# Gate and up projections of the feed-forward sublayers: pairs of inner tiles from seven products of halves, with weight sums formed by ScalarE and an adding DMA

## The chip, the cores and the metric

The kernel runs on one core of a Trainium2 chip. The metric is the time of one execution on the device in microseconds (us). Engines have these names in the profile: PE (TensorE, matmuls), PEld (TensorE's weight loads), DVE (VectorE), ACT (ScalarE), POOL (GpSimd) and SP (SyncE, which issues nearly all DMAs here).

## The reference, cut to what matters

Two layers work on 512 tokens with a model width of 1024. Each layer is a SwiGLU feed-forward sublayer, a token mixer (two kinds of attention and a convolution), and a second SwiGLU sublayer. All is in 32-bit floats.

```python
def swiglu(h, w_up, w_down):
    gate, up = jnp.split(h @ w_up, 2, axis=-1)
    return (jax.nn.silu(gate) * up) @ w_down
...
for l in range(DEPTH):                                   # 2
    mod = (einsum('bd,de->be', silu(c), w_ada[l]) + b_ada[l]).reshape(b, 9, d)
    h = modulate(rmsnorm(x, norm_g[l, 0]), mod[:, 0], mod[:, 1])
    x = x + 0.5 * mod[:, 2][:, None] * swiglu(h, w_ffn_in[l, 0], w_ffn_out[l, 0])
    ...                                                  # token mixer
    h = modulate(rmsnorm(x, norm_g[l, 2]), mod[:, 6], mod[:, 7])
    x = x + 0.5 * mod[:, 8][:, None] * swiglu(h, w_ffn_in[l, 1], w_ffn_out[l, 1])
```

The width inside a feed-forward sublayer is 2816: 22 inner tiles m of 128 channels, each with a gate and an up half. `c` is constant, so `mod` is 72 vectors of 128 channels a layer.

## The kernel before

**Stages.** The program runs the sublayers one after the other. They are called here FFN 1 (with the setup, to about 402 us), mixer 1 (to 994), FFN 2 (to 1370), FFN 3 (to 1745), mixer 2 (to 2331) and FFN 4 (to the end). FFN 2 and FFN 3 follow each other, the last of layer 0 and the first of layer 1.

**A product.** Every operand is kept as two parts, hi and lo, in the format fp32r, and every product is three matmuls into one PSUM bank: hi by hi (L196), weight lo by activation hi (L198), weight hi by activation lo (L200). A feed-forward "unit" is one half (gate or up) of one inner tile m: eight slices k of the width, so 24 matmuls of 512 columns (the tokens), with a 128x1024 block of weights.

**The weights' pipeline.** `plan` yields the keys of the weight blocks in the order of use. `load` lets SP issue the block's DMA into `wr` (512 KB; tag wraw, 3 buffers), makes hi `wh` on ScalarE (L171) and lo `wl` on VectorE (L175), 3 buffers each. `weight` keeps two blocks ahead of the one in use. All of it stands in the program's order: an engine takes its instructions in that order, and a scheduler doesn't move them.

**A feed-forward sublayer.** `norm_h` makes `hh`/`hl` (hi and lo of the normalized input, eight tiles each) at the end of the sublayer before. `head` runs the first three units by halves of the tokens (256 columns). `finish` applies silu on ScalarE (L465), multiplies on VectorE (L466) and splits the product (L190, L191) for the down projection. The inner tiles are taken in three groups (`GROUPS`: 8, 7, 7); after the first tile of the next group the group's down projection runs, eight blocks d, each added to x by `residual` (L420). `tail` does the last group; its last two tiles d run by token halves, so that the next norm lies beside them.

**Other work beside it.** `ada` (L353) makes one vector of `mod` from a 512 KB block: a DMA on SP and one VectorE instruction. 56 of these jobs of layer 0 run in FFN 1, and the 72 of layer 1 belong to FFN 2 (`ada1`), where up to four stand behind each inner tile; in the trace they lie earlier, at about 800 to 990 us in mixer 1, since engines that have nothing else to do there reach them.

Of the kernel before, what the change touches and what calls it, by code (L numbers as in the profile page):

```python
# [13 lines left out]
F32 = mybir.dt.float32  # L14
# [6 lines left out]
P = 128  # L21
T = 512
D = 1024
KD = 8
L = 2
FT = 22
GROUPS = ((0, 8), (8, 15), (15, 22))
# [45 lines left out]
class Trunk:  # L73
    def __init__(self, tc, ctx, io, stop):
# [33 lines left out]
    def plan(self, stop):  # L108
        """Keys of the weight units in the order of their use."""
        n = 0  # L110
        for l in range(L):
            for s in range(3):
# [12 lines left out]
                else:  # L125
                    f = s // 2
                    pend = None
                    if n == 1:
                        yield from (("first", k) for k in range(KD))
                    for m in range(3 if n == 1 else 0, FT):  # L130
                        yield ("in", l, f, m, 0)
                        yield ("in", l, f, m, 1)
                        if pend is not None:
                            yield from (("down", l, f, pend, d) for d in range(KD))
                        pend = {GROUPS[0][1]: 0, GROUPS[1][1]: 1}.get(m + 1)
                    yield from (("down", l, f, 2, d) for d in range(KD))
# [20 lines left out]
    def load(self):  # L157
        key = next(self.keys, None)
        if key is None:
            return  # L160
        nc = self.nc
        src, n = self.source(key)
        kind = key[0]
        raw = self.wp.tile([P, 1024], F32, tag="wraw", name=self.name("wr"), bufs=3)
        hi = self.wp.tile([P, 1024], F32R, tag="whi", name=self.name("wh"), bufs=3)
        lo = self.wp.tile([P, 1024], F32R, tag="wlo", name=self.name("wl"), bufs=3)
        r = raw[:, :n]
        if len(src.shape) == 3:
# [7 lines left out]
        self.loaded.append((key, hi, lo))  # L176
# [222 lines left out]

    def norm_h(self, l, s, k, pb, rng, between=None):  # L400
# [56 lines left out]
    def ffn(self, l, f, ada, cb, stats, nxt, first=None):  # L457
# [3 lines left out]
        start = 0  # L461
# [20 lines left out]
        pend = None  # L482
        early = []
        for m in range(start, FT):
            if m == 0:
                early = self.head(lambda j: self.weight("in", l, f, j // 2, j % 2))
            ps = []
            for j in range(2):
                if early:
                    ps.append(early.pop(0))  # L490
                    continue
                w = self.weight("in", l, f, m, j)
                ps.append(self.bank("mm"))
                self.mmk(ps[j], w, self.h, range(KD), 0, KD - 1)
# [531 lines left out]
```

## Time and profile before

| what | value |
|---|---|
| time of the runs | 2712.62 us median of 3 (2711.9 to 2713.2) |
| span of the profiled execution | 2710.6 us |
| PE busy | 2598.4 us (96%) |
| PEld busy | 2123.6 us (78%) |
| DVE busy | 1612.7 us (59%) |
| ACT busy | 903.2 us (33%) |
| POOL busy | 352.4 us (13%) |
| data moved | 311.27 MB, 115 GB/s on average |

The span runs from the profiled execution's first instruction to its last and is the only time that the profile has of that execution; it is 2.0 us below the median of the runs. Busy shares are averages over stages that differ: the feed-forward sublayers are almost all matmuls, the mixers mix matmuls with much VectorE and GpSimd work. Row groups further down give the stages apart.

### The profile page before, as it was taken

How to read it: one execution, taken by the hardware profiler on the slowest of the kernel's cores; microseconds unless marked ns; L12 is line 12 of the kernel's file. 1: busy time of each engine (PE TensorE's matmuls, PEld its weight loads, DVE VectorE, ACT ScalarE, POOL GpSimd, SP SyncE). 2: the span in 40 equal slices, each digit the busy share in tenths (PEclk: the TensorE clock that was granted, in tenths of full speed). 3: DMA queues.
4: the chain of work that ended last, by engine and by line, in shares of the span. 5: the costliest groups of instructions: out<-in, count | busy, mean ns of one | idle time of the engine just before them, and what ended most of it. 6: DMA issues, size and time to landing. Idle time of an engine off the chain costs nothing.

```text
span 2710.6 us, 31579 instructions
## 1 busy us (share of the span) xinstructions
PE 2598.4 (96%) x12288; PEld 2123.6 (78%) x12288; DVE 1612.7 (59%) x3000; ACT 903.2 (33%) x1490; POOL 352.4 (13%) x289
## 2 busy tenths in 40 slices
PE   7999998689999999999999999977999999999999
PEld 5888887568877788888888888866787778888887
DVE  8883349987868983333353333599878634633333
ACT  3222232245562333222232222322456423422221
POOL 3000004990000000000000000069700000000000
PEclk9999999899999999999999999987999999999999
DMA  7872224222238843223322223221221223222222
GB/s 282 303 286 93 95 92 118 62 62 62 71 101 317 315 166 109 93 90 97 94 86 95 96 90 97 82 70 55 63 67 66 78 93 98 90 93 93 92 95 86
DMA packets 97576, 311.27 MB, mean 115 GB/s; under 512 B 10330, under 2 KB 17242, under 8 KB 97427
## 3 DMA queue, kind: packets, MB, share of 16 engines
q1 hardware_dynamic: 97280, 309.13, 34.3%
q8 instruction: 96, 1.57, 0.2%
q14 instruction: 54, 0.43, 0.1%
q10 hardware_dynamic: 146, 0.14, 0.0%
HBM read 307.09 MB, written 6.06 MB: 116 GB/s over the span
## 4 chain that ended last, share of the span: by engine, by line
PE 83%; DVE 13%; DMA 2%; issue 1%; ACT 1%; SPq 0%; ACTq 0%; DVEq 0%
PE mm L200 24%; PE mm L196 24%; PE mm L198 24%; DVE ca L564 3%; PE mm L634 2%; PE mm L630 2%; PE mm L632 2%; PE s L693 2%; DVE wl L175 2%; DMA ada<-in_w_ada 1%; PE o L762 1%; PE s L735 1%; DVE ada L353 1%; DVE hx L406 1%; DVE rs L235 1%
## 5 line engine op out<-in xcount | busy, mean ns | idle before, releaser
L175 DVE TENSOR_TENSOR wl<-wr,wh 128x1024 fp32r<-128x1024 f32 (+2 forms) x429 | 514.9, 1201 | 475.3 <-ACT wh L171 473.1
L198 PE MATMUL mm<-hh,wl 128*128 128x512 f32 (+1 forms) x2024 | 774.5, 383 | 1.9 <-DVE wl L175 1.8
L196 PE MATMUL mm<-hh,wh 128*128 128x512 f32 (+1 forms) x2024 | 773.2, 383 | 2.4 <-ACT hh L408 2.1
L200 PE MATMUL mm<-hl,wh 128*128 128x512 f32 (+1 forms) x2024 | 767.9, 383 | 6.5 <-DVE hl L411 6.2
L171 ACT ACTIVATE wh<-wr 128x1024 fp32r<-128x1024 f32 (+2 forms) x442 | 444.6, 1006 | 907.6 <-issue 407.2
L200 PEld LDWEIGHTS mm<-hl,wh 128*128 128x128 f32 x2024 | 377.9, 188 | 91.0 <-DVE hl L411 9.7
L198 PEld LDWEIGHTS mm<-hh,wl 128*128 128x128 f32 x2024 | 380.2, 188 | 87.1 <-DVE wl L175 5.4
L196 PEld LDWEIGHTS mm<-hh,wh 128*128 128x128 f32 x2024 | 379.7, 188 | 85.9 <-ACT hh L408 3.5
L196 PE MATMUL mm<-ah,wh 128*128 128x512 f32 (+1 forms) x760 | 288.8, 380 | 0.0
L198 PE MATMUL mm<-ah,wl 128*128 128x512 f32 (+1 forms) x760 | 288.7, 380 | 0.0
L200 PE MATMUL mm<-al,wh 128*128 128x512 f32 (+1 forms) x760 | 288.2, 379 | 0.0
L420 DVE SCALAR_TENSOR_TENSOR x<-mm,res,x 128x512 f32<-128x512 f32 (+1 forms) x124 | 86.2, 698 | 255.3 <-PE mm L200 255.2
L630 PE MATMUL mm<-wh,hh 128*128 128x384 f32 x512 | 188.8, 369 | 39.4 <-DVE v L640 22.2
L175 POOL TENSOR_TENSOR wl<-wr,wh 128x768 fp32r<-128x768 f32 (+1 forms) x13 | 30.5, 2347 | 1456.7 <-ACT wh L171 1456.7
L632 PE MATMUL mm<-wl,hh 128*128 128x384 f32 x512 | 188.1, 367 | 0.0
L634 PE MATMUL mm<-wh,hl 128*128 128x384 f32 x512 | 186.0, 364 | 0.0
L466 DVE TENSOR_TENSOR sil<-sil,mm 128x512 f32<-128x512 f32 x87 | 59.7, 687 | 212.0 <-PE mm L200 210.6
L353 DVE SCALAR_TENSOR_TENSOR ada<-ada,cb 128x1024 f32<-128x1024 f32 x144 | 174.7, 1231 | 17.0 <-DMA ada<-in_w_ada 16.2
L567 POOL TENSOR_TENSOR ca<-ca,prod 128x512 f32<-128x512 f32 x120 | 174.9, 1457 | 9.8
L196 PEld LDWEIGHTS mm<-ah,wh 128*128 128x128 f32 x760 | 143.1, 188 | 30.0
L198 PEld LDWEIGHTS mm<-ah,wl 128*128 128x128 f32 x760 | 143.1, 188 | 29.9
L200 PEld LDWEIGHTS mm<-al,wh 128*128 128x128 f32 x760 | 143.1, 188 | 29.8
(172 smaller groups left out, 2961.6 us busy)
## 6 DMA issues: line engine op xcount, KB each, us to landing
wr<-in_w_ffn_in SPq DMA_DIRECT2D x170, 512.0 KB, 3.3
ada<-in_w_ada SPq DMA_DIRECT2D x144, 512.0 KB, 6.6
wr<-in_w_down SPq DMA_DIRECT2D x64, 448.0 KB, 3.3
wr<-in_w_qkv SPq DMA_DIRECT2D x64, 384.0 KB, 3.2
wr<-in_w_gate SPq DMA_DIRECT2D x48, 512.0 KB, 3.3
wr<-in_w_down SPq DMA_DIRECT2D x32, 512.0 KB, 3.3
wr<-in_w_branch SPq DMA_DIRECT2D x24, 512.0 KB, 3.6
wr<-in_w_u SPq DMA_DIRECT2D x16, 512.0 KB, 3.4
```

Of the source, the lines that this page charges most:

```text
L171: nc.scalar.activation(hi[:, :n], raw[:, :n], AF.Copy)
L175: eng.tensor_tensor(lo[:, :n], raw[:, :n], hi[:, :n].bitcast(F32), op=ALU.subtract)
L196: nc.tensor.matmul(ps[:, rng], w[0][:, wcol], ah[:, rng], start=start, stop=False)
L198: nc.tensor.matmul(ps[:, rng], w[1][:, wcol], ah[:, rng], start=False, stop=False)
L200: nc.tensor.matmul(ps[:, rng], w[0][:, wcol], al[:, rng], start=False, stop=stop)
L353: nc.vector.scalar_tensor_tensor(w, w, 1.0, cb, op0=ALU.mult, op1=ALU.mult, accum_out=self.mod[l][:, e:e + 1])
L420: self.nc.vector.scalar_tensor_tensor(self.x[d][:, rng], ps[:, rng], self.res[l][:, 8 * s + d:8 * s + d + 1], self.x[d][:, rng], op0=ALU.m ...
L564: eng.scalar_tensor_tensor(ca[j], u, w, ca[j], op0=ALU.mult, op1=ALU.add)
L567: eng.tensor_tensor(ca[j], ca[j], prod, op=ALU.add)
L630: nc.tensor.matmul(o, hi[:, hs], w[0][:, ws], start=k == 0, stop=False)
L632: nc.tensor.matmul(o, hi[:, hs], w[1][:, ws], start=False, stop=False)
L634: nc.tensor.matmul(o, lo[:, hs], w[0][:, ws], start=False, stop=k == KD - 1)
```

## The change

The matrix product of two inner tiles (a "pair" j, tiles 2j and 2j+1) is taken as a 2x2 product of blocks: tokens in two halves, the width in two halves of four slices k, and gate against up. It is then formed from seven products of half size and sums (the Winograd form of Strassen's scheme) instead of eight:

- Each product is 2 tiles x 4 slices x 3 parts = 24 matmuls of 256 columns (`product`). A pair had 96 matmuls of 512 columns and has 168 of 256.
- The weight blocks 11, 21, 12, 22 (gate and up, each with the lower and upper half of the width, for both tiles) have 128x1024 elements. Products 1, 2, 3 use blocks 11, 21, 22 as loaded by SP. Products 5, 7, 6, 4 use t1 = 12 - 11, t3 = 12 - 22, t2 = 22 - t1, t4 = 21 - t2. For each of these four `less` writes the negated first operand with ScalarE (L251), and a DMA issued by POOL adds the other block from memory onto it (L252).
- The activations' sums S1 to S4 are made once a sublayer (`sums`, VectorE L555 to L561, splits L267 and L268) from unsplit copies `hq` of the normalized input, which `norm_h` now writes as well (a ScalarE instruction of 256 columns for each tile and half).
- In `pair`, three intermediate values are copied out of PSUM on ScalarE (L599) and three sums are taken on VectorE; then silu (L626, L629), products and splits for both tiles together.
- The products run in the order 1, 2, 6, 7, 5, the next pair's 1, 3, 4. The next pair's blocks are therefore loaded, negated and added during products 7 to 4 of the pair before, or, at a group's end, during the down projection.
- FFN 1 keeps its tiles 0 to 3 as they were and has 9 pairs; FFNs 2 to 4 keep tiles 0 and 1 and have 10 pairs each: 39 pairs in all. The groups are 8, 8 and 6 tiles.
- Space: wraw has 5 buffers instead of 3; t1, t2, `hq` and the `ada` blocks share 4 double buffers with the convolution's tiles. Of the 72 jobs of `ada1`, 40 stay in FFN 2 (up to two after each pair, plain tile or down tile) and 32 move to FFN 3. The split of the convolution's output moves to the end of the mixer.

```diff
-GROUPS = ((0, 8), (8, 15), (15, 22))
+GROUPS = ((0, 8), (8, 16), (16, 22))
+ORDER = (1, 2, 6, 7, 5, 3, 4)
...
+    def block(self, l, f, j, p):
+        if p == 1:
+            self.pairs[j] = b = {}
+            src = {q: self.io["w_up"][l, f, j, i] for i, q in enumerate((11, 21, 12, 22))}
+            for q in (11, 21, 22):
+                b[q] = self.raw()
+                self.nc.sync.dma_start(b[q], src[q])
+            self.less(b, "t1", self.z4k("t"), b[11], src[12])
+            self.less(b, "t3", self.raw(), b[22], src[12])
+            self.less(b, "t2", self.z4k("t"), b["t1"], src[22])
+            self.less(b, "t4", self.raw(), b["t2"], src[21])
+        return self.pairs[j][{1: 11, 2: 21, 6: "t2", 7: "t3", 5: "t1", 3: 22, 4: "t4"}[p]]
+
+    def less(self, b, name, out, a, src):
+        self.nc.scalar.activation(out, a, AF.Copy, scale=-1.0)
+        self.nc.gpsimd.dma_start(out, src, accum_op=ALU.add)
+        b[name] = out
...
+        if s != 1:
+            for half in range(2):
+                if rng in (FULL, HALF[half]):
+                    nc.scalar.activation(self.quarter(k, half), hx[:, HALF[half]], AF.Identity, bias=b)
...
+    def sums(self):
+        tt = self.nc.vector.tensor_tensor
+        a11, a12, a21, a22 = (self.quarters[q] for q in (11, 12, 21, 22))
+        self.S = {}
+        def keep(n, t):
+            self.S[n] = (self.t4k([P, D], F32R, "sh"), self.t4k([P, D], F32R, "sl"))
+            self.split(self.S[n], t)
+        tt(a22, a21, a22, op=ALU.add)
+        tt(a21, a21, a11, op=ALU.subtract)
+        tt(a11, a22, a11, op=ALU.subtract)
+        keep(2, a11)
+        keep(3, a21)
+        keep(1, a22)
+        tt(a12, a12, a11, op=ALU.subtract)
+        keep(4, a12)
...
+    def product(self, l, f, j, p, bank, first):
+        nc = self.nc
+        w = self.weight("up", l, f, j, p)
+        acts = self.operand(p)
+        for mi in range(2):
+            o = bank[:, mi * 256:mi * 256 + 256]
+            for k in range(4):
+                c = slice((mi * 4 + k) * P, (mi * 4 + k + 1) * P)
+                for x, (a, b) in enumerate(((0, 0), (1, 0), (0, 1))):
+                    nc.tensor.matmul(o, w[a][:, c], acts[k][b], start=first and (mi, k, x) == (0, 0, 0),
+                                     stop=(k, x) == (3, 2), skip_group_check=True)
+
+    def pair(self, l, f, j, st, nxt, acts):
...
+        if 1 not in st:
+            run(st, j, 1, "mm")
+        snap("c11")
+        run(st, j, 2, "s")
+        tt(st["c11"], st["c11"], st[2], op=ALU.add)
+        more(6)
+        snap("u2")
+        run(st, j, 7, "s")
+        more(5)
+        snap("c22")
+        tt(st["c22"], st["c22"], st[7], op=ALU.add)
+        later = {}
+        if nxt is not None:
+            run(later, nxt, 1, "mm")
+        more(3)
+        self.product(l, f, j, 4, st[7], False)
...
```

Where the instructions now stand, at two places. First ScalarE's queue in FFN 4. Before, in the steady part, a tile m has two weight splits, one silu and one split of the result:

```order
L465 ACTIVATE sil_3475_20228<-mm_3470_20172 128x512
L171 ACTIVATE wh_3479_20236<-wr_3478_20235 128x1024
L171 ACTIVATE wh_3483_20267<-wr_3482_20266 128x1024
L190 ACTIVATE ah_3476_20231<-sil_3475_20228 128x512
L465 ACTIVATE sil_3486_20297<-mm_3481_20241 128x512
```

Of the change, the stretch from pair 2 to pair 3. Here `wr_3515` is pair 3's block 11, `t_3518` and `t_3520` are its t1 and t2, and `wh_3507`, `wh_3509`, `wh_3513` are the hi parts for pair 2's products 6, 7 and 5:

```order
L599 ACTIVATE c11_3505_21886<-mm_3495_21791 128x512
L224 ACTIVATE wh_3507_21889<-t_3490_21754 128x1024
L251 ACTIVATE t_3518_21983<-wr_3515_21977 128x1024
L224 ACTIVATE wh_3509_21918<-wr_3489_21751 128x1024
L629 ACTIVATE u2_3481_21711<-u2_3481_21711 128x512
L251 ACTIVATE t_3520_21989<-t_3518_21983 128x1024
L267 ACTIVATE ah_3503_21882<-act_3502_21876 128x1024
L224 ACTIVATE wh_3513_21949<-t_3488_21748 128x1024
```

What moved: between the weight splits of one pair there now stand two negations of the next, and the second (`t_3520<-t_3518`) reads what the DMA has added onto the first; the split for product 5 is queued behind it.

Second, the start of FFN 4. On ScalarE, behind the head, `sh` are hi parts of the sums, `wr_3461` is pair 1's block 11, `t_3464`, `t_3466`, `wr_3467` its t1, t2 and t4, and the last row is the hi part for product 6:

```order
L267 ACTIVATE sh_3454_21554<-hq_3434_21360 128x1024
L251 ACTIVATE t_3464_21576<-wr_3461_21570 128x1024
L267 ACTIVATE sh_3456_21559<-hq_3417_21236 128x1024
L599 ACTIVATE c11_3475_21651<-mm_3472_21622 128x512
L267 ACTIVATE ah_3459_21566<-sil_3471_21617 128x512
L251 ACTIVATE t_3466_21582<-t_3464_21576 128x1024
L251 ACTIVATE wr_3467_21585<-t_3466_21582 128x1024
L224 ACTIVATE wh_3477_21654<-t_3466_21582 128x1024
```

On VectorE at the same place, from the last `hl` of the norm on, with the sums on the `hq` tiles and their lo parts `sl`:

```order
L499 SCALAR_TENSOR_TENSOR hl7_97<-hx_3437_21373,shift1_110,hh7_96 128x256
L555 TENSOR_TENSOR hq_3434_21360<-hq_3429_21339,hq_3434_21360 128x1024
L556 TENSOR_TENSOR hq_3429_21339<-hq_3429_21339,hq_3412_21215 128x1024
L228 TENSOR_TENSOR wl_3446_21393<-wr_3444_21390,wh_3445_21392 128x1024
L557 TENSOR_TENSOR hq_3412_21215<-hq_3434_21360,hq_3412_21215 128x1024
L645 TENSOR_TENSOR sil_3458_21563<-sil_3458_21563,mm_3448_21397 128x512
L561 TENSOR_TENSOR hq_3417_21236<-hq_3417_21236,hq_3412_21215 128x1024
L228 TENSOR_TENSOR wl_3469_21589<-wr_3461_21570,wh_3468_21588 128x1024
L268 TENSOR_TENSOR sl_3451_21547<-hq_3412_21215,sh_3450_21546 128x1024
L268 TENSOR_TENSOR sl_3453_21551<-hq_3429_21339,sh_3452_21550 128x1024
```

What moved: t1 takes over the memory of a tile `hq`, so its negation waits until VectorE has read that tile for the last time (the first `sl`), and t2's negation waits for t1's DMA. Before the change VectorE had nothing there between `hl7` and the split of a weight.

## Rows read from the trace of the kernel before

**Rows 1.** The page's first part: span, and busy time of the engines.

```profile
span 2710.6 us, 31579 instructions
PE 2598.4 (96%) x12288; PEld 2123.6 (78%) x12288; DVE 1612.7 (59%) x3000; ACT 903.2 (33%) x1490; POOL 352.4 (13%) x289
```

**Rows 2.** Busy by stretch: us, PE, PEld, DVE, ACT, POOL, clock, DMA share, GB/s.

```profile
994.00:1370.00 376.00, 375.48 (x1736) 307.02 (x1735) 148.32 (x210) 105.33 (x140) 3.16 (x2) 1.00 0.29 93
...
2331.00:2710.60 379.60, 375.22 (x1733) 306.75 (x1731) 142.10 (x186) 99.33 (x130) 2.40 (x1) 1.00 0.28 92
```

**Rows 3.** Waits of PE in FFN 4 (2331 to 2711).

```profile
PE mm L200 <- DVE hl L411: 0.3, 1, 0.3
```

**Rows 4.** Timeline of DVE in FFN 3, down projection.

```profile
1481.23 0.75 DVE L420 SCALAR_TENSOR_TENSOR x<-mm,res,x 128x512 f32<-128x512 f32 x1 [2.64 <-PE mm L200]
...
1486.85 0.75 DVE L420 SCALAR_TENSOR_TENSOR x<-mm,res,x 128x512 f32<-128x512 f32 x1 [3.26 <-PE mm L200]
```

**Rows 5.** Timeline of DVE at the end of FFN 4, by token halves.

```profile
2699.41 0.48 DVE L420 SCALAR_TENSOR_TENSOR x<-mm,res,x 128x256 f32<-128x256 f32 x1 [1.72 <-PE mm L200]
2701.88 0.48 DVE L420 SCALAR_TENSOR_TENSOR x<-mm,res,x 128x256 f32<-128x256 f32 x1 [1.98 <-PE mm L200]
```

**Rows 6.** Timeline of ACT behind the head of FFN 3.

```profile
1387.08 0.92 ACT L408 ACTIVATE hh<-hx,shift 128x256 fp32r<-128x256 f32 x2 [1.05 <-DVE hx L406]
1389.17 1.06 ACT L171 ACTIVATE wh<-wr 128x1024 fp32r<-128x1024 f32 x1 [1.18 <-PE mm L200]
1390.13 0.58 ACT L465 ACTIVATE sil<-mm 128x512 f32<-128x512 f32 x1
1390.61 1.05 ACT L171 ACTIVATE wh<-wr 128x1024 fp32r<-128x1024 f32 x1
```

**Rows 7.** Timeline of DVE behind the head of FFN 3.

```profile
1387.62 0.89 DVE L411 SCALAR_TENSOR_TENSOR hl<-hx,shift,hh 128x256 fp32r<-128x256 f32 x2 [0.19 <-ACT hh L408]
...
1392.00 1.22 DVE L175 TENSOR_TENSOR wl<-wr,wh 128x1024 fp32r<-128x1024 f32 x1
1393.14 0.69 DVE L191 TENSOR_TENSOR al<-sil,ah 128x512 fp32r<-128x512 f32 x1
1393.78 1.23 DVE L175 TENSOR_TENSOR wl<-wr,wh 128x1024 fp32r<-128x1024 f32 x1
```

**Rows 8.** Busy time in a stretch of mixer 1 with many ada loads.

```profile
900.00:950.00 50.00, 50.00 (x215) 40.04 (x214) 46.39 (x74) 15.92 (x21) 0.37 (x3) 1.00 0.89 322
```

**Rows 9.** DMA issues: count, KB each, median us from issue to landing.

```profile
wr<-in_w_ffn_in SPq DMA_DIRECT2D x170, 512.0 KB, 3.3
ada<-in_w_ada SPq DMA_DIRECT2D x144, 512.0 KB, 6.6
...
wr<-in_w_ffn_in SPq DMA_DIRECT2D x8, 384.0 KB, 9.2
```

**Rows 10.** Timeline of PE where the head of FFN 3 ends.

```profile
1391.31 0.28 PE L200 MATMUL mm<-hl,wh 128*128 128x256 f32 x1
1391.42 0.39 PE L196 MATMUL mm<-hh,wh 128*128 128x512 f32 x1
```

**Rows 11.** Timeline of PE in mixer 1, the first matmuls after an idle time.

```profile
492.65 0.66 PE L630 MATMUL mm<-wh,hh 128*128 128x384 f32 x1 [11.42 <-DVE v L640]
493.10 0.53 PE L632 MATMUL mm<-wl,hh 128*128 128x384 f32 x1
...
496.30 0.47 PE L634 MATMUL mm<-wh,hl 128*128 128x384 f32 x1
...
496.78 0.34 PE L632 MATMUL mm<-wl,hh 128*128 128x384 f32 x1
496.96 0.34 PE L634 MATMUL mm<-wh,hl 128*128 128x384 f32 x1
```

**Rows 12.** Busy time in the stretch of these matmuls, columns as in rows 2.

```profile
492.00:496.00 4.00, 3.35 (x11) 3.38 (x12) 4.00 (x14) 0.00 (x0) 3.73 (x4) 0.50 0.35 98
```

**Rows 13.** Weight loads of TensorE, grouped by line and shape.

```profile
L198 PEld LDWEIGHTS mm<-hh,wl 128*128 128x128 f32 x2024 | 380.2, 188 | 87.1 <-DVE wl L175 5.4 <-issue 0.4
```

More of the change, by code (lines that the diff above doesn't have):

```diff
@@ L83, in __init__ @@
         self.uid = 0
+        self.spare = None
+        self.ready = False
+        self.zspare = None
+        self.pairs = {}
         self.keys = self.plan(stop)
+        self.quarters = {}
         self.loaded = deque()
@@ L125, in plan, with ffn_blocks, ffn_plan @@
                 else:
[L126 to L136, printed above, removed]
+                    yield from self.ffn_plan(n, l, s // 2)
                 if n == stop:
                     return
+    def ffn_blocks(self, n):
+        plain = 4 if n == 1 else 2
+        out = [("plain", m) for m in range(3 if n == 1 else 0, plain)]
+        pend = None
+        for j in range(plain // 2, FT // 2):
+            out.append(("pair", j))
+            if pend is not None:
+                out.append(("down", pend))
+            pend = {GROUPS[0][1]: 0, GROUPS[1][1]: 1}.get(2 * j + 2)
+        return out
+    def ffn_plan(self, n, l, f):
+        if n == 1:
+            yield from (("first", k) for k in range(KD))
+        blocks = self.ffn_blocks(n)
+        early = False
+        for (kind, i), nxt in zip(blocks, blocks[1:] + [("end", 0)]):
+            if kind == "plain":
+                yield ("in", l, f, i, 0)
+                yield ("in", l, f, i, 1)
+            elif kind == "down":
+                yield from (("down", l, f, i, d) for d in range(KD))
+            else:
+                for p in ORDER:
+                    if p == 1 and early:
+                        continue
+                    if p == 3 and nxt[0] == "pair":
+                        yield ("up", l, f, nxt[1], 1)
+                    yield ("up", l, f, i, p)
+                early = nxt[0] == "pair"
+        yield from (("down", l, f, 2, d) for d in range(KD))
     def source(self, key):
@@ new lines, in pair, with run, snap, more @@
+    def pair(self, l, f, j, st, nxt, acts):
+        nc = self.nc
+        tt = nc.vector.tensor_tensor
+        def run(st, j, p, tag, first=True):
+            if first:
+                st[p] = self.bank(tag)
+            self.product(l, f, j, p, st[p], first)
+        def snap(name):
+            st[name] = self.t2k(name)
+            nc.scalar.activation(st[name], st[1], AF.Copy)
+        def more(p):
+            self.product(l, f, j, p, st[1], False)
+        if 1 not in st:
[14 more added lines that the diff above has]
+        self.product(l, f, j, 4, st[7], False)
+        act = self.t4k([P, 2, T], F32, "act")
+        halves = [act[:, :, h] for h in HALF]
+        def two(t):
+            return t.rearrange("p (a b) -> p a b", a=2)
+        nc.scalar.activation(st["c11"], st["c11"], AF.Silu)
+        tt(halves[0], two(st["c11"]), two(st[1]), op=ALU.mult)
+        tt(st["u2"], st["u2"], st[7], op=ALU.add)
+        nc.scalar.activation(st["u2"], st["u2"], AF.Silu)
+        tt(halves[1], two(st["u2"]), two(st["c22"]), op=ALU.mult)
+        hi, lo = self.act_tiles("a")
+        self.split((hi, lo), act)
+        for i in range(2):
+            acts[2 * j + i] = (hi[:, i, :], lo[:, i, :])
+        return later
@@ L471, in unit, with more @@
             return lambda d: self.weight("down", l, f, g, d)
+        def more(k):
+            for _ in range(k):
+                if ada:
+                    ada.popleft()(cb)
         if first:
-            start = 3
             banks = [self.bank(t) for t in ("mm", "mm", "mm", "mm", "s", "s")]
```

155 lines of the change are left out of this document (100 added, 55 removed).

## The prediction

> **What bounds the kernel now.** The first view is the page's busy time: PE is busy 2598.4 of 2710.6 us and the other engines far less [rows 1]. Such a share is an average, so the second view is the busy time by sublayer: in FFN 2 PE works 375.48 of 376.00 us, in FFN 4 375.22 of 379.60, at the full clock, while ACT works about 100 us, DVE 142 to 148 and the DMA engines 0.28 of the time [rows 2]. The third is the list of PE's waits: 0.3 us in FFN 4 [rows 3]. The feed-forward sublayers are a gapless stream of matmuls. Each us of PE taken out is gained, as long as nothing else becomes late; each us by which a weight or a sum comes late is lost in full, since nothing covers it.
>
> The profiled execution has no time of its own beside its span, 2710.6; the median of the runs, 2712.6, lies 2.0 above. I work out differences from the trace and take them from the median.
>
> **What is removed.** One `residual` of the down projection follows the next after 1486.85 - 1481.23 = 5.62 us [rows 4], the time of 24 matmuls of 512 columns. In the tail's token halves the step is 2701.88 - 2699.41 = 2.47 us for 7 x 3 = 21 matmuls of 256 columns [rows 5]: 0.1174 us each against 0.2341, just half. A product of 24 costs 24 x 0.1174 = 2.82 us. A pair took 4 x 5.62 = 22.48 and will take 7 x 2.82 = 19.72: 2.76 us less, and for 39 pairs **107.6 us** less. Both counts come from shapes that the trace has; this term is firm.
>
> **What is added, in steady pairs.** By busy time nothing overflows: for each pair ACT does 12 instructions of 128x1024 (seven hi parts, four negations, one split) at 1.0 us and five of 512 columns at 0.5 [rows 6], 14.6 us; DVE eight at 1.15 and five at 0.6 [rows 7], 12.2 us; both under 19.72. DMA: 900:950 moves 322 GB/s at a share of 0.89 [rows 8], so 512 KB occupy all engines for 1.45 us; three plain loads and four adding ones, each counted twice since the target is read too, make 11 x 1.45 = 16.0 of 19.72.
>
> But the order of ACT's queue forms a loop. The second negation of the next pair (t2) needs what the DMA put into t1, and the hi part for product 5 stands behind it. Around the loop: hi part for product 6 (1.0), negate t1 (1.05), DMA (D), negate t2 (1.05), split of the result (1.0), hi part for product 5 (1.0), its lo part (1.15), products 5, 1, 3 (8.45) until the buffer for the next hi part 6 is free: **14.7 + D**. Against 19.72 PE waits once D exceeds 5.0. The loop runs at 15 transitions between pairs (1 to 2, 2 to 3, 3 to 4, 7 to 8 in FFNs 2 to 4; three of FFN 1); at the others one of a group's eight down tiles (5.62 us each) lies between the negations. Loss: 15 x (D - 5.0), not below 0.
>
> **D, the unknown price.** The trace has no adding DMA and none issued by POOL. From below, a plain load of 512 KB: 3.3 us from issue to landing; from above, the slowest load, 9.2 [rows 9]. I start at 3.3, add 1.45 for reading the target and 0.7 for half of another load on the same engines: **D = 5.4**, between the rows 3.3 and 6.6 (the `ada` loads, several in flight), the two nearest.
>
> *A page on this.* The Trainium skill, "Collectives: The Full Stack", section on the bandwidth ceiling (fold count), says that an add in the DMA path costs no computing time, but a second source read (measured ratio 62.28 to 32.35). No run here shows it. By it alone D would be about 3.3 + 1.45 = 4.75, an estimate, and the sum below 2658; I keep the 0.7 of sharing.
>
> **What is added, at the four starts.** Here nothing has run ahead, and the chain is serial. FFN 4, counted from the end of the last `hl` (1388.51 for FFN 3 [rows 7]): DVE does L555 and L556 (2.3), a weight's lo part (3.45), L557 (4.6), a silu product (5.2), L561 (6.35), the lo part of product 1 (7.5), the first lo of a sum (8.65). Then `hq` is free and ACT negates t1 (9.7); it lands at 9.7 + D; t2 negated 10.75 + D, landed 10.75 + 2D; t4 negated, hi and lo part of product 6: **14.0 + 2D**. PE ends the head 1391.42 - 1388.51 = 2.9 us after the last `hl` [rows 7, 10], then runs the fourth unit (5.62) and products 1 and 2 (5.64): ready for product 6 at 14.2. Loss 2D - 0.2. By the same count in the other queues: FFN 2, where t1 waits for the third lo part (2.3 later), 2D + 2.1; FFN 3, with an `ada` instruction between, 2D + 2.6; FFN 1, where tile 3's two units stand between, 2D - 1.6. Sum **8D + 2.9** = 46.1.
>
> Two smaller terms belong to these starts. The extra `hq` instruction on ACT (0.46, as each of the two `hh` [rows 6]) makes ACT's 0.92 a tile as long as DVE's own; its last copies delay the final `hl` by between 0 and eight times 0.46; I take 1.2 for three norms, **3.6**. And PE will stand still for about 10 us: after an idle time of 11.42 [rows 11] the trace shows a granted clock of 0.50 [rows 12], the 1.2 GHz level, with matmuls of 384 columns 0.32 apart, where later ones are 0.18 apart [rows 11]. Some 3.85 us at half speed lose 1.9; four times, **7.6**; nothing if the idle times stay too short for it.
>
> **What is moved.** `ada` blocks now take turns with t1 and t2 for four buffers. While down tiles run, a DMA or negation may wait for a VectorE instruction of `ada`: 0 to 5 us in all, I take **3**. In mixer 1 fewer `ada` jobs compete (900:950 has PE full as it is [rows 8]), but the convolution's late split is added at a place that DVE reaches with work to spare: taken as 0, bounds 2 gained, 4 lost. Five raw buffers and SP's queue cost nothing: loads take 3.3 us [rows 9] against products of 2.82 with two blocks ahead, and only three of seven blocks come through SP.
>
> **Sum.** 107.6 - 46.1 - 3.6 - 7.6 - 15 x 0.4 (6.0) - 3 = 41.3 gained: 2712.6 - 41.3 = **2671**. In general the gain is 107.6 - 17.1 - 8D - 15 x (D - 5.0), the last where D is over 5. D = 3.3 gives 64.1 (2648; 2641 with the clock kept), D = 6.6 gives 13.7 (2699), and nothing is left at D = 7.2.
>
> **Rivals.**
>
> *The adding DMA is cheap* (D up to 4.5, the steady loop never waits): 2636 to 2655. For it: the plain load's 3.3; against it: twice the traffic, and two to three other loads under way at a start.
>
> *The adding DMA is dear, and the change loses.* From D = 7.2 on, the loop and the starts eat up the saved matmuls. At 9.2 the loss is 8 x 9.2 + 17.1 + 15 x 4.2 - 107.6 = 46: 2759. The same comes if its transfers use engines for longer than two plain ones: four times three reads' worth would make (3 + 12) x 1.45 = 21.8 us a pair, over 19.72, 39 x 2.1 = 82 us more. For it: 9.2 and 6.6 in this trace, where loads queue [rows 9]; against it: FFNs use 0.28 of the DMA engines [rows 2], so that there is room.
>
> *The halved matmuls don't halve.* Were the spacing bound by the weight load, 188 ns each [rows 13], a pair would take 168 x 0.188 = 31.6 us, 9.1 more than now: 2712.6 + 39 x 9.1 = 3068. Against it stand 21 such matmuls in 2.47 us, 0.117 apart with a load each [rows 5]. The Trainium skill, "TensorE: Matmul & The Clock Gate", section "Back-to-back issue gap", says that load and matmul together set the spacing, about 81 ns at 128 columns and 131 at 512; by that line (98 at 256, an estimate) half the columns cost 0.75 of the time, and a pair 29.3 us. The trace disagrees: 0.50.
>
> *No change* (within 0.2%, 5.4 us, which is what a measurement of this kernel can tell): D from 7.0 to 7.4, or a smaller D with the mixers a little worse.
>
> **How the numbers follow.** D between 4.5 and 6.1, with the bounds of the small terms: 0.43, time 2655 to 2690, likeliest 2671. Cheap adds (2636 to 2655): 0.18. D near 6.6 (2690 to 2707): 0.13. No change (2707 to 2718): 0.07. Slower: 0.19, of which 0.17 for the dear DMA (a third of it below 2725) and 0.02 for the spacing. The range 2640 to 2730 leaves out about 0.04 below and 0.14 above. The forecast's own range is 2655 to 2690. Faster 0.74, same 0.07, slower 0.19.
>
> **What would show it.** In the profile after: 256-column matmuls about 0.117 apart; PE busy lower by about 108 us; in each sublayer one idle time of some 10 us ahead of product 6, its releaser the lo part behind two DMAs in a row, and a lower clock behind it; adding DMAs of 5 to 6 us; and in the steady pairs waits of under 1 us at the hi part for product 5. Wrong would be: landings of 7 us or more, or DMA engines near full in the pairs; PE waiting in every pair, those after down tiles too; or mixers longer by more than 4 us.

## The result and the profile after

The changed kernel takes 2798.2 us (median of 4 runs, 2789.9 to 2801.4) against 2712.9 of the kernel before: a ratio of 1.0306, 95% interval 1.0289 to 1.0324. It is **slower by 3.1%**; the forecast was 2671 us, 1.5% faster, with a range of 2640 to 2730. The profiled execution spans 2796.5 us, 85.9 more than before.

The page's first part answers to [rows 1]:

```profile
span 2796.5 us, 38523 instructions
PE 2564.0 (92%) x15072; PEld 2243.4 (80%) x15072; DVE 1835.8 (66%) x3227; ACT 1271.5 (45%) x1921; POOL 473.1 (17%) x445
```

PE's busy time fell by 34 us, not by 108, and its idle time rose from 112 to 232 us. Where, is read from the busy time by stretch (columns as in [rows 2]): FFN 1; mixer 1; FFNs 2, 3 and 4 each in two parts, up to the end of the first product 6 ("start") and from there on ("pairs"), with mixer 2 between them:

```profile
0.00:427.50 427.50, 377.82 (x2299) 336.17 (x2300) 294.66 (x437) 199.63 (x247) 50.72 (x61) 0.97 0.76 217
427.50:1009.90 582.40, 547.32 (x2743) 450.79 (x2742) 420.34 (x934) 243.38 (x475) 157.10 (x130) 0.96 0.28 82
1009.90:1062.00 52.10, 38.68 (x255) 35.84 (x254) 39.53 (x75) 32.16 (x53) 4.54 (x6) 0.88 0.48 123
1062.00:1420.80 358.80, 331.05 (x2185) 304.83 (x2185) 213.24 (x278) 166.62 (x193) 31.48 (x36) 0.97 0.70 183
1420.80:1475.40 54.60, 40.64 (x254) 37.78 (x253) 40.65 (x77) 32.48 (x56) 5.51 (x6) 0.85 0.46 114
1475.40:1822.40 347.00, 328.72 (x2186) 301.95 (x2185) 204.35 (x260) 165.58 (x192) 31.85 (x40) 0.97 0.69 177
1822.40:2402.80 580.40, 538.55 (x2739) 443.26 (x2738) 421.00 (x931) 240.03 (x472) 157.05 (x130) 0.98 0.25 75
2402.80:2452.50 49.70, 36.71 (x255) 33.88 (x254) 34.95 (x67) 32.12 (x53) 4.63 (x6) 0.90 0.39 84
2452.50:2796.50 344.00, 324.52 (x2175) 298.90 (x2173) 167.08 (x174) 159.48 (x182) 30.27 (x35) 0.98 0.56 132
```

FFN 2 takes 411 us (375 before), FFN 3 402 (375), FFN 4 394 (377), FFN 1 427.5 (403); the mixers became shorter, 582 and 580 us (593 and 587 before). Each start has PE idle for 13 to 14 us; but in the pairs, where the forecast had nearly nothing, PE is idle for 28, 18 and 19 us, and the granted clock is under 1.00 in all feed-forward stretches, which had it at 1.00 before.

PE's waits in the pairs of FFN 4 (2452.5 to the end), against 0.3 us in [rows 3]:

```profile
PE mm L583 <- ACT u L599: 12.0, 4, 4.3
PE mm L583 <- ACT c L599: 3.2, 4, 1.2
```

The largest wait is for `u`, the copy of a PSUM bank into `u2` on ScalarE, which must be made before product 5 adds to that bank. ScalarE's timeline shows why it is late, from pair 3's start to the copy for its product 5:

```profile
2486.80 0.60 ACT L599 ACTIVATE c<-mm 128x512 f32<-128x512 f32 x1 [0.94 <-PE mm L583]
2487.29 1.05 ACT L224 ACTIVATE wh<-wr 128x1024 fp32r<-128x1024 f32 x1
...
2494.62 1.06 ACT L251 ACTIVATE t<-wr 128x1024 f32<-128x1024 f32 x1 [1.06 <-DMA wr<-in_w_up]
...
2502.13 1.06 ACT L251 ACTIVATE t<-t 128x1024 f32<-128x1024 f32 x1 [4.98 <-DMA t<-in_w_up]
2503.09 1.04 ACT L267 ACTIVATE ah<-act 128x1024 fp32r<-128x1024 f32 x1
2504.04 1.04 ACT L224 ACTIVATE wh<-t 128x1024 fp32r<-128x1024 f32 x1
2504.99 0.61 ACT L626 ACTIVATE c<-c 128x512 f32<-128x512 f32 x1
2505.51 0.58 ACT L599 ACTIVATE u<-mm 128x512 f32<-128x512 f32 x1
```

The other engines' timelines give the steps between (DVE, SP, POOL, and PE at the two ends):

```profile
2481.48 0.58 PE L583 MATMUL mm<-sh,wh 128*128 128x256 f32 x1 [4.28 <-ACT u L599]
...
2488.38 1.23 DVE L228 TENSOR_TENSOR wl<-wr,wh 128x1024 fp32r<-128x1024 f32 x1 [0.26 <-ACT wh L224]
...
2489.63 2.67 SPq L240 DMA_DIRECT2D wr<-in_w_up  x2
...
2495.98 0.86 POOL L252 DMA_DIRECT2D t<-in_w_up  x1 [8.96 <-ACT t L251]
...
2506.13 0.38 PE L583 MATMUL mm<-sh,wh 128*128 128x256 f32 x1 [2.26 <-ACT u L599]
```

Read in order: product 5 of a pair starts (2481.48); 5.3 us later ScalarE copies c22, another of the three values that leave PSUM, and makes the hi part for product 4, VectorE its lo part; that frees a raw buffer, and only then SP issues the load of the next pair's block 11 (2489.63); it lands 5.0 us later and t1 is negated (2494.62); POOL issues the adding DMA (2495.98), which lands 6.1 us later; t2 is negated (2502.13); and behind it stand the split, the hi part for product 5 (2504.04), a silu and the copy `u`. Product 5 of the next pair starts at 2506.13. The loop takes **24.65 us**.

What a wait does to the clock stands in the busy time by stretch around the first of these waits (columns as above):

```profile
2478.00:2482.00 4.00, 0.52 (x2) 0.36 (x2) 2.36 (x2) 4.00 (x6) 0.86 (x1) 0.66 0.41 52
2482.00:2486.00 4.00, 4.00 (x20) 4.00 (x20) 2.36 (x2) 3.44 (x4) 0.86 (x1) 0.50 0.41 81
2486.00:2490.00 4.00, 4.00 (x35) 4.00 (x35) 1.92 (x2) 1.92 (x3) 0.86 (x1) 0.99 0.79 139
```

PE waits 4.28 us, during which the granted clock falls, and then works 4 us at 0.50 (1.2 GHz): 20 matmuls instead of 35.

The DMA part answers to [rows 9]:

```profile
wr<-in_w_up SPq DMA_DIRECT2D x117, 512.0 KB, 4.6
wr<-in_w_up POOLq DMA_DIRECT2D x78, 512.0 KB, 5.6
t<-in_w_up POOLq DMA_DIRECT2D x78, 512.0 KB, 5.8
```

### The profile page after: what moved, and what is told of

It reads as the page before. It is cut to its first block, busy times and chain, and to the rows that moved or that the text cites. A ratio compares the mean times of both kernels' runs of the same rounds, so it can differ in the third digit from the quotient of the medians.

```text
span 2796.5 us, 38523 instructions
## 1 busy us (share of the span) xinstructions
PE 2564.0 (92%) x15072; PEld 2243.4 (80%) x15072; DVE 1835.8 (66%) x3227; ACT 1271.5 (45%) x1921; POOL 473.1 (17%) x445
## 3 DMA queue, kind: packets, MB, share of 16 engines
q1 hardware_dynamic: 91808, 289.20, 31.7%
q0 software_dynamic: 22464, 81.80, 17.5%
q8 instruction: 118, 1.93, 0.3%
## 4 chain that ended last, share of the span: by engine, by line
PE 56%; issue 18%; DVE 14%; DMA 8%; ACT 3%; POOL 1%; POOLq 0%; DVEq 0%; ACTq 0%
PE mm L273 11%; PE mm L277 11%; PE mm L275 11%; PE mm L583 6%; PE s L583 5%; DMA t<-in_w_up 4%; DMA ada<-in_w_ada 3%; DVE ca L757 3%; DVE wl L228 3%; PE mm L823 2%; PE mm L827 2%; PE mm L825 2%; PE s L886 2%; DVE ada L430 1%; DMA wr<-in_w_up 1%
## 5 line engine op out<-in xcount | busy, mean ns | idle before, releaser
L228 DVE TENSOR_TENSOR wl<-wr,wh 128x1024 fp32r<-128x1024 f32 (+1 forms) x468 | 557.1, 1195 | 397.1 <-ACT wh L224 395.9
L224 ACT ACTIVATE wh<-wr 128x1024 fp32r<-128x1024 f32 (+1 forms) x481 | 481.1, 1007 | 496.9 <-PE mm L277 205.4
L583 PE MATMUL mm<-sh,wh 128*128 128x256 f32 x936 | 285.4, 305 | 90.3 <-ACT u L599 44.1
L583 PE MATMUL mm<-sh,wl 128*128 128x256 f32 x936 | 283.3, 303 | 5.1 <-DVE wl L228 4.8
L275 PE MATMUL mm<-hh,wl 128*128 128x512 f32 (+1 forms) x776 | 280.9, 365 | 5.2 <-DVE wl L228 5.2
L273 PE MATMUL mm<-hh,wh 128*128 128x512 f32 (+1 forms) x776 | 280.7, 365 | 2.8 <-ACT hh L492 2.7
L277 PE MATMUL mm<-hl,wh 128*128 128x512 f32 (+1 forms) x776 | 275.5, 366 | 5.6 <-DVE hl L499 5.2
L583 PE MATMUL mm<-sl,wh 128*128 128x256 f32 x936 | 280.0, 299 | 0.0
L252 POOL DMA_DIRECT2D t<-in_w_up x78 | 67.5, 865 | 883.0 <-ACT t L251 832.8
L583 PEld LDWEIGHTS mm<-sh,wl 128*128 128x128 f32 x936 | 195.3, 209 | 8.4 <-DVE wl L228 8.3
L583 PEld LDWEIGHTS mm<-sl,wh 128*128 128x128 f32 x936 | 196.0, 209 | 0.0
L583 PE MATMUL s<-hh,wl 128*128 128x256 f32 x624 | 177.6, 285 | 20.1 <-DVE wl L228 20.1
```

What stands on the lines that cost most here:

```text
L228: eng.tensor_tensor(lo[:, :n], raw[:, :n], hi[:, :n].bitcast(F32), op=ALU.subtract)
L273: nc.tensor.matmul(ps[:, rng], w[0][:, wcol], ah[:, rng], start=start, stop=False)
L275: nc.tensor.matmul(ps[:, rng], w[1][:, wcol], ah[:, rng], start=False, stop=False)
L277: nc.tensor.matmul(ps[:, rng], w[0][:, wcol], al[:, rng], start=False, stop=stop)
L583: nc.tensor.matmul(o, w[a][:, c], acts[k][b], start=first and (mi, k, x) == (0, 0, 0), stop=(k, x) == (3, 2), skip_group_check=True)
```

## The experiments

Theory A: PE waits for the serial path (load, negation, adding DMA, negation) and for what stands behind a waiting negation in ScalarE's queue; the waits also cost clock. Rivals: B, the amount of work and of transfers; C, the seven products themselves. Each kernel starts from the changed one, and its ratio is to the kernel before.

**e1_plain: no sums of weights.** Left out: negations and adding DMAs; the t blocks hold a plain block, so the results are other ones.

```diff
-        self.nc.scalar.activation(out, a, AF.Copy, scale=-1.0)
-        self.nc.gpsimd.dma_start(out, src, accum_op=ALU.add)
+        self.nc.sync.dma_start(out, src)
```

> The four weight sums are left out: t1 to t4 are plain loads of blocks by SP, without negations and adding DMAs; the rest of the change stays. Theory A (PE waits for the serial path negate, adding DMA, negate, and for what is queued behind it on ScalarE; each wait also costs clock): no waits in the pairs, no stretch at half clock in the feed-forward sublayers, 2600 to 2630 us, since 107.6 of matmuls and about 17 in the mixers are then gained in full. Theory B (the DMA engines or ScalarE have too much to do): the same. Theory C (the seven products themselves are dear: short matmuls, changes of bank, copies out of PSUM): the waits or the slow clock stay, 2700 or more.

2654.5 us, ratio 0.978 (0.976 to 0.980). So C falls as the cause, and making the sums costs 144 us. But it was 25 us above what I expected. A part of that is in the starts; FFN 3's takes 47.5 us, with PE busy for 38.5:

```profile
1342.50:1390.00 47.50, 38.52 (x255) 36.18 (x254) 40.89 (x77) 27.62 (x51) 1.13 (x1) 0.86 0.46 155
```

PE waits there for lo parts of weights, 6.4 us in one place. VectorE makes them, and in between S1 to S4 and their lo parts, whatever the weights do.

**e2_flat: as many negations and adding DMAs, none in series.** Other sums than the reference's: t2 and t4 negate loaded blocks.

```diff
-            self.less(b, "t2", self.z4k("t"), b["t1"], src[22])
+            self.less(b, "t2", self.z4k("t"), b[21], src[22])
-            self.less(b, "t4", self.raw(), b["t2"], src[21])
+            self.less(b, "t4", self.raw(), b[22], src[21])
```

> As many negations on ScalarE and adding DMAs as in the change, but t2 and t4 negate loaded blocks (21 and 22) instead of t1 and t2, so no negation waits for an adding DMA; the sums are other ones. Theory A: the waits at the copy u2 and behind it nearly vanish; at the four starts one DMA remains in the path instead of two, about 5 us each: 2620 to 2680 us. Theory B (number of transfers and of ScalarE instructions): unchanged within 20 us of 2798.

2748.5 us, ratio 1.0125 (1.0105 to 1.0146), 50 us less than the change and between the two forecasts: A is half right here. FFN 4's pairs:

```profile
2423.40:2747.20 323.80, 317.72 (x2174) 293.30 (x2173) 167.70 (x174) 157.78 (x181) 29.34 (x34) 1.00 0.60 138
```

323.8 instead of 344.0 us at full clock, with the same DMAs: B falls for FFN 4. FFN 2 went only from 411 to 401, so there something else is at work.

**e3_pool_sums: GpSimd subtracts, all four blocks loaded plainly.**

```diff
-            self.less(b, "t1", self.z4k("t"), b[11], src[12])
...
+            c = self.raw()
+            self.nc.sync.dma_start(c, src[12])
+            sub = lambda o, x, y: self.nc.gpsimd.tensor_tensor(o, x, y, op=ALU.subtract)
...
+            sub(b["t1"], c, b[11])
+            sub(b["t2"], b[22], b["t1"])
+            sub(c, c, b[22])
...
+            sub(b["t4"], b[21], b["t2"])
```

> The four sums are made by GpSimd from four plainly loaded blocks, no negation and no adding DMA; all else as in the change. A subtraction of 128x1024 is estimated at 2.9 us from the 1.46 us of one of 128x512 (L567 of the kernel before), in a queue of its own. Theory A: no waits in the steady pairs, at the starts two subtractions in a row cost 2 to 4 us each: 2610 to 2660 us. Against it: if GpSimd is slowed by VectorE to 4.9 us or more, four of them exceed the 19.7 us of a pair, and it comes out at 2700 or more.

2819.7 us, ratio 1.0387 (1.0371 to 1.0402): a miss. GpSimd took 2.5 to 3.3 us an instruction, near the estimate, 11.5 a pair. What I had not counted was VectorE; this is its group of lo parts in FFN 4's pairs (by line and shape; first the change, then this kernel):

```profile
L228 DVE TENSOR_TENSOR wl<-wr,wh 128x1024 fp32r<-128x1024 f32 x63 | 76.6, 1224 | 61.6 <-ACT wh L224 61.5
```

```profile
L228 DVE TENSOR_TENSOR wl<-wr,wh 128x1024 fp32r<-128x1024 f32 x63 | 104.7, 1672 | 32.1 <-ACT wh L224 32.1
```

The mean of 1.67 us mixes two kinds: the 44 lo parts that ran beside no GpSimd instruction took 1.22 us as before, the 19 that overlapped one took 1.23 to 3.40, 2.71 on the mean. PE now waits for lo parts most. In FFN 4's pairs that is 11 us, and they still take 336 us against the change's 344. The loss is in the other sublayers, FFN 3 above all (418 us against 402), where PE waits 43 us for lo parts; VectorE has the `ada` work there too, and what each of the two adds was not separated.

**e4_staged: ScalarE in the order of the text**, t1 negated two products earlier, t2 and t3 later, t4 later still.

```diff
...
+        with self.tc.manual_schedule(engines={mybir.EngineType.Activation}):
...
+        if p == 7 and self.chained(j + 1):
+            self.stage(l, f, j + 1, 1)
...
+        if p == 3 and self.chained(j + 1):
+            self.stage(l, f, j + 1, 3)
+            self.stage(l, f, j + 1, 5)
+        if p == 2 and direct:
+            self.stage(l, f, j, 4)
```

> The same instructions as the change, in another order: ScalarE issues in the order of the text in the feed-forward sublayers, and between pairs t1 is negated two products earlier and t2, t3 behind the copy u2, t4 later still. Theory A: the waits at the copy u2 vanish in the steady pairs with the slow clock behind them, the starts stay as they are (about 11 us and a slow stretch each): 2650 to 2700 us. Theory B: as many transfers and as much work on ScalarE, so 2780 to 2800.

2985.7 us, ratio 1.100 (1.098 to 1.102): a clear miss. The waits at `u` are gone, but PE waits for hi parts instead, which the text has behind the silu and the split of the pair before (FFN 4's pairs):

```profile
PE mm L610 <- ACT wh L224: 20.7, 16, 2.1
PE mm L610 <- DVE wl L228: 7.1, 9, 1.2
```

That doesn't test A alone, because all of ScalarE's order changed. It shows that an order of the same instructions can cost 187 us.

**f1_hold: two edges of order, nothing else.** `hold` is the last copy out of PSUM: `u2` where t2's negation is issued, c22 where t4's is.

```diff
+            with self.behind():
+                self.less(b, "t2", self.z4k("t"), b["t1"], src[22])
...
+        if p == 2 and "t4" not in self.pairs[j]:
+            b = self.pairs[j]
+            with self.behind():
+                self.less(b, "t4", self.raw(), b["t2"], self.io["w_up"][l, f, j, 1])
...
+    def behind(self):
+        return self.tc.issue_after(self.hold) if self.hold else nullcontext()
...
+            done = nc.scalar.activation(st[name], st[1], AF.Copy).ins
+            self.hold = done if nxt is not None else None
```

> The same instructions as the change with two edges of order: t2's negation for the next pair is issued behind the copy u2, t4's behind the copy c22. Theory A (ScalarE's order: what stands behind a negation that waits for an adding DMA makes PE wait): PE's waits in FFN 4's pairs fall from 16 us to about 3, as where the sums were independent (e2_flat), in the others from 68 to about 55; with half of the slow time gone, 2735 to 2770 us. Rival B (the path of two DMAs is too long wherever it stands): the waits move to products 6 and 4, 2785 to 2820.

2737.0 us, ratio 1.0082 (1.0062 to 1.0102): 61 us less than the change, with every instruction and every byte kept. Between pairs, the built order now has the hi part for product 5, the split and `u` ahead of t2's negation (in FFN 4's pair 3 at 2450.56, 2452.03 and 2453.51, t2 at 2455.18). FFN 4's pairs take 324.2 us at full clock; below them stand the busy times of the whole span:

```profile
2410.30:2734.50 324.20, 317.12 (x2175) 293.10 (x2173) 167.74 (x174) 160.54 (x182) 30.26 (x35) 1.00 0.60 140
```

```profile
PE 2543.3 (93%) x15072; PEld 2228.7 (82%) x15072; DVE 1836.4 (67%) x3227; ACT 1273.1 (47%) x1921; POOL 472.5 (17%) x445
```

A holds for the pairs. None of PE's 44.1 us of waits for `u` is left in the whole span, and the waits did not move elsewhere: those for hi parts, lo parts and c in the products rise from 78 to 83 us.

**f2_plain4: four plain tiles ahead of the pairs.**

```diff
-        plain = 4 if n == 1 else 2
+        plain = 4
```

> Four plain tiles ahead of the pairs in every feed-forward sublayer instead of two (36 pairs instead of 39), so PE has 22.5 us more of work while the sums are made. If the starts' idle time is the serial path from the sums through two adding DMAs: about 40 us of waits and some 20 us of slow clock in FFNs 2 to 4 go, 8 us of saved matmuls are given back: 2735 to 2765 us. If the starts wait for work that is only queued later as well: 2790 or more.

2761.1 us, ratio 1.017 (1.014 to 1.020). FFN 4's start loses 4 us instead of 13, but those of FFNs 2 and 3 still 13 and 14 (PE busy 60.3 of 73.3 and 63.3 of 77.2 us): there something besides the serial path holds them up. In g1_best below, where FFNs 2 and 3 hold no `ada` jobs, they lose 5 and 7 us in all.

**f3_ada_mixer: the ada jobs of layer 1 in mixer 1**, in 4 KB buffers, behind its convolution.

```diff
...
+        for br, y in ((1, yb), (2, yc)):
+            for i, _ in enumerate(self.gates(l, br, y, z, False)):
+                if l == 0 and i % 8 == 7:
+                    for _ in range(2 if i % 16 == 7 else 1):
+                        if self.mix_jobs:
+                            self.mix_jobs.popleft()(cb)
...
```

> The 72 ada jobs of layer 1 are put into mixer 1 behind its convolution, in the 4 KB buffers that they had before the change; FFNs 2 and 3 hold none. Theory A with a second part (VectorE waits in its queue for an ada load, and lo parts behind it): the pairs of FFNs 2 and 3 lose about as much as those of FFN 4, 16 us each instead of 28 and 18, their slow time falls too: 2765 to 2785 us, mixer 1 longer by 0 to 11 us. If ada has no part in it: 2795 to 2810.

2812.3 us, ratio 1.036 (1.034 to 1.038). FFNs 2 and 3 fell to 393 us each, by 26 us together, but mixer 1 rose by 41:

```profile
424.90:1047.80 622.90, 556.73 (x2742) 456.40 (x2741) 502.86 (x1091) 243.07 (x475) 157.09 (x130) 0.94 0.41 138
```

**f4_all: the three edits together.**

> The three edits together (order of t2 and t4, four plain tiles, ada in mixer 1). If the three causes are separate, their gains add up to 100 to 120 us: 2670 to 2710 us, faster than the kernel before. If they share the same waits: 2730 to 2750.

2702.2 us, ratio 0.9958 (0.9942 to 0.9975): 0.4% faster than the kernel before, although mixer 1 still takes 624 us. FFNs 2 to 4 take 358, 363 and 362.

**g1_best: as f4_all, with the ada jobs in the text ahead of FFN 2**, so that the build spreads them over mixer 1.

```diff
...
+                    if n == 3:
...
+                        while ada1:
+                            ada1.popleft()(cb)
```

> Order of t2 and t4 and four plain tiles as in f4_all, but the 72 ada jobs of layer 1 stand ahead of FFN 2 in the text, in 4 KB buffers, so that the build spreads them over mixer 1 as before the change. f4_all lost 41 us in mixer 1 (624 us); if that was the place of the jobs, mixer 1 takes 582 to 595 us and the whole 2660 to 2680; if mixer 1 cannot take them beside the change's mixer, 2690 to 2705.

2664.0 us, ratio **0.9816** (0.9801 to 0.9830): the best kernel of this study, 1.8% faster than before. Mixer 1 takes 584 us with all 72 jobs. FFNs 2, 3 and 4:

```profile
996.60:1355.60 359.00, 354.37 (x2366) 323.80 (x2365) 204.26 (x260) 190.55 (x236) 32.61 (x38) 1.00 0.58 137
1355.60:1718.10 362.50, 355.89 (x2366) 325.25 (x2365) 206.02 (x263) 191.31 (x239) 33.88 (x42) 1.00 0.58 135
...
2298.90:2660.60 361.70, 353.83 (x2355) 323.66 (x2353) 198.01 (x236) 184.27 (x226) 31.42 (x37) 0.99 0.56 133
```

These pairs run without a wait, so they give the bare price of one (PE's timeline in FFN 4, first matmul of product 5 in three pairs that follow each other):

```profile
2467.59 0.28 PE L593 MATMUL mm<-sh,wh 128*128 128x256 f32 x1
...
2487.59 0.28 PE L593 MATMUL mm<-sh,wh 128*128 128x256 f32 x1
...
2507.59 0.28 PE L593 MATMUL mm<-sh,wh 128*128 128x256 f32 x1
```

20.00 us a pair.

**g2_two: f1 and f2 together, ada as in the change.**

> Order of t2 and t4 and four plain tiles; ada as in the change. The two gained 61 and 37 us alone; if they act at separate places, 2690 to 2710 us together; if the starts' and the pairs' waits are the same ones, 2720 to 2740.

2694.1 us, ratio 0.9926 (0.9906 to 0.9946): the two add up. FFNs 2 and 3 take 377 and 376 us, against 359 and 362.5 in g1_best, where ada is the only difference: 32 us.

**g3_yc: the convolution's output split early again.**

```diff
...
-            nc.vector.tensor_tensor(y, ca[j], sg, op=ALU.mult)
-            self.yc.append(y)
+            nc.vector.tensor_tensor(ca[j], ca[j], sg, op=ALU.mult)
+            a = self.act_pair("yc")
+            self.split(a, ca[j])
+            self.yc.append(a)
...
```

> The change with one part undone: the convolution's output is split inside the convolution again, not at the end of the mixer. If that part made the mixers shorter (593 to 582 and 587 to 580 us), both return to about 590 and the time is 2810 to 2820; if it was another part (buffers), 2790 to 2805.

2800.2 us, ratio 1.032 (1.029 to 1.034). The mixers take 586 and 584 us, 3.5 us more each: a third of mixer 1's gain and half of mixer 2's. Where the rest comes from I didn't try.

**g4_down: g2_two, in FFNs 2 and 3 with no ada behind a pair.**

```diff
                 st = self.pair(l, f, i, st, after[1] if after[0] == "pair" else None, acts)
-                more(2)
+                if n == 1:
+                    more(2)
```

> g2_two with the ada jobs of FFNs 2 and 3 behind down tiles and plain tiles alone, none behind a pair. If VectorE's waits for ada loads hold up the lo parts in the pairs, the pairs of FFNs 2 and 3 come down to FFN 4's 4 us and it is 10 to 25 us faster than g2_two; if not, the same within 5 us.

2693.7 us, ratio 0.9929 (0.9912 to 0.9946): no different from g2_two. So ada's price does not come from standing behind the pairs. Whether it is the shared buffers, the transfers or VectorE's queue was not separated.

## Why the prediction was wrong

The sum, term by term, from the trace of the change, but for the 20.00 us of a bare pair, which g1_best gives. FFNs: idle time is the stretch less PE's busy time. The clock's term is half of the time that PE worked at 0.50 there, 104.6 us of the 126 at that clock; the whole span has 198 us at 0.50 (its mean granted clock is 0.965), 72 of them in the mixers.

| term | forecast | measured |
|---|---|---|
| saved matmuls | -107.6 | -96.7 (39 x (22.48 - 20.00)) |
| starts, idle and extra hq | +49.7 | +47.8 (13.4 + 14.0 + 13.0 + 7.4; FFN 1 less the 20 us that it had before) |
| pairs, idle (15 transitions, ada) | +9.0 | +84.6 (22.4 + 27.7 + 18.3 + 16.2 for FFNs 1 to 4; FFN 4 without its end, behind the last matmul) |
| clock | +7.6 | +52.3 |
| mixers | 0 | -17.3 |
| sum | -41.3 | +70.7; 15.2 of 85.9 not placed, PE's busy time by the rows |

**Right: the halved matmuls.** Spacing is 0.117 to 0.120 us; only 0.28 us a pair is missing, 10.9 in all. The rival of the weight load falls. The 0.75 that was estimated from the Trainium skill, "TensorE: Matmul & The Clock Gate", section "Back-to-back issue gap", disagrees with this too: 20.00 / 168 against 5.62 / 24 us is 0.51.

**Nearly right: D.** The median landing is 5.6 and 5.8 us after issue where 5.4 was forecast, and POOL issues 0.3 us after the negation. So D as the sum uses it, from the negation's end on, is 5.9 to 6.1, and 6.0 to 6.5 at the places shown here. By the sum's own formula 6.5 gives 2697 us, so this alone doesn't make the change lose. (By that formula D = 4.75 gives 2660, not 2658.) The rival of the dear DMA gave the right sign for the wrong reason: the median landings stayed well under its 7.2, and an adding DMA holds the engines no longer than two plain ones. By queue:

```profile
q1 hardware_dynamic: 91808, 289.20, 31.7%
q0 software_dynamic: 22464, 81.80, 17.5%
```

POOL's 156 adding DMAs take 17.5% of 2796.5 us, 3.1 us each; SP's take 31.7% for 289.2 MB, 1.6 us for 512 KB. That is a ratio of 1.95. What the Trainium skill, "Collectives: The Full Stack", section on the bandwidth ceiling, says of the second source read agrees with it: measured there, 62.28 to 32.35, or 1.93.

**Right, with one part missing: the starts.** The last `hl` on VectorE and ScalarE's timeline in FFN 4's start:

```profile
2420.76 0.48 DVE L499 SCALAR_TENSOR_TENSOR hl<-hx,shift,hh 128x256 fp32r<-128x256 f32 x1 [0.32 <-ACT hh L492]
```

```profile
2430.33 1.05 ACT L251 ACTIVATE t<-wr 128x1024 f32<-128x1024 f32 x1
...
2437.88 1.06 ACT L251 ACTIVATE t<-t 128x1024 f32<-128x1024 f32 x1 [3.45 <-DMA t<-in_w_up]
2444.95 1.06 ACT L251 ACTIVATE wr<-t 128x1024 f32<-128x1024 f32 x1 [6.00 <-DMA t<-in_w_up]
2445.91 1.04 ACT L224 ACTIVATE wh<-t 128x1024 fp32r<-128x1024 f32 x1
```

The last `hl` ends at 2421.24. t1 is negated 9.1 us later, where 8.65 was forecast, and the hi part for product 6 begins 24.7 us later, where 11.75 + 2 x 5.4 = 22.6 was forecast: two adding DMAs in a row, which land 6.5 and 6.0 us after the negations. But the idle time is not one, as forecast. Ahead of product 6 PE waits 25.1 us at all four starts together:

```profile
PE mm L583 <- ACT wh L224: 25.1, 4, 7.7
```

Before that it waits 5.2, 6.6 and 2.9 us in FFNs 2 to 4 for the lo part of product 1 or 2. These waits stay without any weight sum (5.9, 6.4 and 2.3 us in e1_plain). So beneath the path through the DMAs lies a second limit, VectorE's queue, which the sum did not have.

**Wrong: the loop of the steady pairs, "14.7 + D. Against 19.72 PE waits once D exceeds 5.0".** This is the step that failed. The forecast loop was 20.1 us; the one shown above takes 24.65. Its path through t1, the DMA, t2 and the hi part for product 5 was right, and three things make it longer. First, I held "five raw buffers and SP's queue" to cost nothing, because a load takes 3.3 us. But the load of block 11 is issued only when product 4's lo part has freed its buffer, 8.2 us after product 5 starts, and lands 5.0 us later; ScalarE stands idle 1.06 us for it before it negates t1 (0.25 to 4.05 us, 32 in all, at the 15 places where PE waits for `u`). Second, products 5, 1 and 3 take 10.8 us instead of 8.45, since the wait has brought the clock down. Third, the DMA lands 6.45 us after the negation, not 5.4. Together that is 4.5 us. The share of the first I have only read from the trace; no run changed the raw buffers alone.

I also stopped at the hi and lo part for product 5. The profile names the copy `u`, another silu and 0.6 us behind the hi part; in the turn shown the lo part comes 0.4 us later still, so `u` adds nothing to the forecast path there, nor at eight other places. At the remaining six, 14 of the 44 us, the parts for product 5 had been ready for 3 to 6 us, and `u` alone stood behind t2's negation. The 15 places cost 44 us, not 6 (PE's waits over the whole span):

```profile
PE mm L583 <- ACT u L599: 44.1, 15, 5.0
```

f1_hold shows what the queue's order costs: two edges that put what product 5 needs ahead of t2's negation gain 61 us, and FFN 4's pairs lose no more than 4 us of waits.

**Wrong: the clock, a term mis-sized.** I charged it four times, once a start, from an idle time of 11.42 us [rows 11]. In this trace most waits of 2 to 5 us are followed by it too. By the granted clock it costs 52 us beside 132 us of idle time. f1_hold gives the price of a wait as a whole: its span is 62.0 us shorter, 41.3 of them idle time and 20.7 PE's busy time (2564.0 to 2543.3, with as many matmuls), half a us for each us of waiting. With the waits gone it goes: g1_best has 1.00 in FFNs 2 and 3 and 0.99 in FFN 4.

**Wrong: ada, a term mis-sized.** 3 us (0 to 5) was forecast; taking ada out of FFNs 2 and 3 gains 30 us (g2_two to g1_best). I had seen the contest for buffers between ada, t1 and t2, but priced it by down tiles alone; which way ada costs PE that time stays open (g4_down).

**Wrong in the section on the kernel.** I wrote that all stands in the order of the text and that a scheduler doesn't move it. The build does reorder: in ScalarE's rows above, the silu of c11 (L626) stands ahead of the copy `u` (L599), which the text has first. The prediction's queues came from the built order, so its sum doesn't hang on this; but it is why an edge of order was the cure. e4_staged shows what ScalarE in the order of the text, with the negations moved, cost.

**The mixers** gave 17.3 us against a bound of 2. Before the change:

```profile
403.20:996.30 593.10, 544.97 (x2743) 448.09 (x2742) 509.08 (x1089) 242.26 (x472) 162.84 (x134) 0.97 0.43 145
...
1746.30:2333.30 587.00, 548.64 (x2738) 452.28 (x2737) 426.67 (x929) 238.37 (x469) 162.28 (x130) 0.95 0.24 74
```

Mixer 1's gain is idle time of PE (48 us before, 35 after); mixer 2's is busy time, with the granted clock at 0.98 instead of 0.95. The late split gives 3.5 of it in each; the rest stays open.

## What to carry to other kernels

When an engine's queue holds an instruction that waits for a DMA, list everything behind it and close a loop through each of them, including the load that the buffer's last reader releases and the lower clock that a wait leaves behind; then compare the longest to the period. Saved matmuls are only worth their time if PE stays fed, since waits here cost one and a half times their length (f1_hold). A change that loses can have a good core: here two edges of order, two plain tiles more and another place for unrelated loads turned +3.1% into -1.8%.

## What the runs showed of the hardware

- In a wait of PE of 4.28 us the granted clock fell to 0.50 and stayed there for the next 4 us of work; all FFN stretches of the change show a mean of 0.85 to 0.98, FFN 4's pairs without these waits (e2_flat, f1_hold) 1.00.
- An adding DMA of 512 KB from POOL lands 5.6 to 5.8 us (medians) after issue and holds the DMA engines for 1.95 times as long as a plain one.
- VectorE's 128x1024 subtractions took 1.22 us beside an idle GpSimd, and 2.71 on the mean (up to 3.40) where they overlapped one of GpSimd's own (e3_pool_sums, FFN 4's pairs).
